# A sixth seven-product piece per group, and low parts made by ScalarE and an adding transfer, in a streaming-encoder block

## The chip, the core and the metric

The kernel runs on one core of a Trainium2 chip. The core has a matrix engine (TensorE, PE in the profile; its weight loads are listed apart as PEld), VectorE (DVE), ScalarE (ACT), GpSimd (POOL) and SyncE (SP). Each takes its own instructions in order, and they wait for each other by semaphores. Transfers between HBM and SBUF, or within SBUF, are issued from a queue of an engine (here SP's, for two small cases ACT's) and are carried by 16 transfer engines. Matmuls accumulate in PSUM, eight banks of 128 x 512 float32. The metric is the device time of one execution in microseconds.

## What is computed

One layer of an encoder on 256 tokens of width 2048, all in float32: a half feed-forward block, a mixer of two recurrent branches, cross-attention to 256 memory tokens, a second half feed-forward block, and a last norm. The change touches the two feed-forward blocks alone:

```python
DFF = 5632
def swiglu(h, w_up, w_down):
    gate, up = jnp.split(h @ w_up, 2, axis=-1)
    return (jax.nn.silu(gate) * up) @ w_down
...
x = x + 0.5 * swiglu(rms_norm(x, ffn1_norm[l]), ffn1_w_up[l], ffn1_w_down[l])
...
x = x + 0.5 * swiglu(rms_norm(x, ffn2_norm[l]), ffn2_w_up[l], ffn2_w_down[l])
return rms_norm(x, final_norm)
```

## The kernel before

**Float32 from two halves.** TensorE multiplies in the rounded type float32r. Every float32 operand v is therefore split into a high part h, v rounded to float32r, and a low part l = v - h. A product is three matmuls: high by high, low by high, high by low; low by low is dropped. `split` (line 119) does this: ScalarE copies v into h, VectorE subtracts h from v into l. `three` (line 421) issues the matmuls of a list of products: first, for each product, the weights' high part with the high and the low part of x; then, for each product, the weights' low part with the high part of x. So the low part of a weight piece is needed last.

**Pieces of weights.** All weights stream from HBM once, in pieces of 128 x 2048 float32, 1 MB. `plan` (line 127) lists them in order; `weights` (line 164) keeps two of them prepared ahead: before the matmuls of a piece are written out, those of the next are already split. `prepare` (line 181) issues the load into a `raw` buffer on SP's queue and then the split. There are three `raw`, three `h` and three `l` buffers (lines 71 to 73), and one `td`, one `tl` and one `ev` in the feed-forward blocks (line 321).

**A feed-forward block** (`ffn`, line 440). The 5632 hidden columns are taken in 11 groups of 512. A group's up projection runs over 8 pieces p; each holds 256 rows (two slices of 128) of 512 gate and 512 up columns, so with the two halves of the 256 tokens it is a 2 x 2 by 2 x 2 block product. `PRODUCTS` (line 433) names how a piece is multiplied:

- "plain" (group 0): the eight ordinary products.
- "fast": seven products of sums of blocks, after Strassen and Winograd. The sums of weight blocks are made by VectorE, three subtractions into `td` (lines 194 to 196), and `td` is split as well, into a second `h` buffer and `tl`. So a fast piece costs VectorE `td`, `l` (1536 wide), and `tl` (two halves of 1024); ScalarE copies 1536 + 2 x 1024.
- "mixed": eight products which add into the same accumulators as the seven-product kind, from the plain weight blocks with two extra operands of x (`less`). It costs the split of 2048 alone.

Both kinds add into seven accumulators, one PSUM bank each. Which product of which piece is the first and the last in an accumulator is in `uses` (line 444). At the end ScalarE and VectorE fold the seven accumulators into gate and up of both token halves and apply silu (lines 496 to 518): first, behind the last fast piece, accumulators 0, 5 and 4, which only fast pieces use (lines 504 to 506); the rest behind the group's last piece. The result is turned by eight transposes and split into two `hidop` tiles (`turn`, line 458), four pieces later.

The down projection of two earlier groups is spread between the groups: four down pieces of 24 matmuls follow each group's up pieces (line 54), adding to the residual `x` at line 532.

`ffn_order` (line 42) lays down the order. In groups 1 and 2 kinds alternate; from group 3 on it is 1, 0, 3, 4, 2, 5, 7, 6 with pieces 0, 2 and 6 mixed and 1, 3, 4, 5 and 7 fast.

**x operands.** For each pair of slices of x, `operand_pairs` (line 384) makes the split of x itself and what the kind needs beside it: `less` for mixed pieces, four sums for pieces of the "fast" kind. Piece 4 is mixed in groups 1 and 2 and fast from group 3 on, so pair 4 needs both sets, and its `less` goes to a slot of its own, `xd`. In the first block this runs at the start, between the first pieces (line 570), in the second between the pieces of the matmul before it.

**Order.** The first eight preparations are in an order written out by hand (`manual_schedule`, line 169). For the rest the compiler orders each engine's instructions by their place in the program and by when it expects their inputs and buffers; buffers are given out at compile time, and the waits are fixed with them.

Of the kernel before, what the change touches and what calls it, by code (L numbers as in the profile page):

```python
# [41 lines left out]
def ffn_order():  # L42

    out, down = [("plain", 0, p) for p in range(8)], [("down", 0, 1, c, 0) for c in range(4)]
    for g in range(1, NG):
        if g < 3:  # L50
            out += [(("mixed", "fast")[p % 2], g, p) for p in (0, 1, 2, 3, 5, 4, 7, 6)]
        else:
            out += [("mixed" if p in (0, 2, 6) else "fast", g, p) for p in (1, 0, 3, 4, 2, 5, 7, 6)]
        if g > 2 and g % 2:
            down = [("down", g - 2, 2, c, b) for c in range(4) for b in (g - 2, g - 1)]
        n = 2 if g < 3 else 4
        out, down = out + down[:n], down[n:]
    return out + [("down", NG - 2, 2, c, b) for c in range(4) for b in (NG - 2, NG - 1)]
# [3 lines left out]
def block_kernel(ctx: ExitStack, tc: tile.TileContext, xT, xin, memT, vec, gfin, bgate, lruw, wu1, wd1, win, wv,  # L62
# [24 lines left out]
    def slot(dt=F32, name="slot"):  # L87
        return slots.tile([P, 1024], dt, name=name, tag="slot")
# [41 lines left out]
    def plan_ffn(name, wu, wd):  # L130
        for e in orders[name]:
            src = wd[e[4], e[3]] if e[0] == "down" else wu[e[1], e[2]]
            plan.append(((name,) + e, src, e[0] == "fast"))

    def plan_columns(name, w, which):
        plan.extend(((name, i), w[i], False) for i in which)

    def plan_rows(name, w, g):
        plan.extend(((name, g, kq), w[g, kq], False) for kq in range(w.shape[1]))

    plan_ffn("ffn1", wu1, wd1)
    for hf in range(2):
# [21 lines left out]
    def weights(*key):  # L164
        while plan and len(ahead) < 2:
            i = next(planned)
            k, src, fast = plan.pop(0)
            if i == 0:
                in_turn.enter_context(tc.manual_schedule(engines={sp.engine, act.engine, dve.engine}))
            if i < len(head):  # L170
                head[i]()
            ahead.append((k, prepare(src, fast, 4 if i < 4 else 1)))
            if i in rest:
                rest[i]()
            if i == 7:
                in_turn.close()
        k, w = ahead.pop(0)
        assert k == key, (k, key)
        return w

    def prepare(src, fast, cuts=1):

        raw = rawp.tile([P, 2048], F32, name="raw", tag="raw")
        n = 2048 // cuts
        if not fast:
            h, l = split_tiles()
            for a in range(0, 2048, n):
                sp.dma_start(raw[:, a:a + n], src[:, a:a + n])
# [5 lines left out]
        dve.tensor_tensor(out=two[0], in0=raw[:, None, :512].broadcast_to([P, 2, 512]), in1=two[1], op=ALU.subtract)  # L194
        dve.tensor_tensor(out=td[:, 1024:1536], in0=raw[:, 1024:1536], in1=td[:, :512], op=ALU.subtract)
        dve.tensor_tensor(out=td[:, 1536:], in0=raw[:, 1536:], in1=td[:, 1024:1536], op=ALU.subtract)
# [184 lines left out]

    def operand_pairs(src, gain, q, xg, out):

        for a in src:
            i = len(out)
            g = xg[:, i * 512:(i + 1) * 512]
            for z in range(2):
                act.activation(g[:, z * T:][:, :T], a[:, z * T:(z + 1) * T], ACT.Copy,  # L390
                               scale=col(gain, 4 * q + 2 * i + z))
            h, l = slot(F32R, "xh"), slot(F32R, "xl")
            split(h[:, :512], l[:, :512], g)
            both = 2 * q + i == 4
            d = slot(F32R, "xd") if both else None
            less = None if i else (d[:, :256], d[:, 256:512]) if both else (h[:, 512:768], l[:, 512:768])
            out.append(((h, l), less))

        def sums():
            s = slot(name="xs")  # L400
            for i, ((h, l), less) in enumerate(out):
                a = [xg[:, i * 512 + j * P:][:, :P] for j in range(4)]

                def made(h, l, n, at, terms):
                    o = [s[:, at + j * P:][:, :P] for j in range(n)]
                    for j, (x, y, op) in enumerate(terms(o)):
                        dve.tensor_tensor(out=o[j], in0=x, in1=y, op=op)
                    split(h, l, s[:, at:at + n * P])

                if less:  # L410
                    made(*less, 2, 0, lambda o: ((a[0], a[1], ALU.subtract), (a[2], a[3], ALU.subtract)))
                if i or 2 * q + i == 4:
                    if not i:
                        s = slot(name="xs")
                    made(h[:, 512:], l[:, 512:], 4, 512 * i,
                         lambda o: ((a[1], a[3], ALU.add), (o[0], a[0], ALU.subtract),
                                    (a[1], a[0], ALU.subtract), (a[2], o[1], ALU.subtract)))

        return sums
# [20 lines left out]
    def ffn(name, pairs, sq, then, begin=(), sums=()):  # L440
# [38 lines left out]
        for at, e in enumerate(order):  # L479
# [3 lines left out]
            if kind != "down":  # L483
# [9 lines left out]
                                     u[0] == (p, i), u[-1] == (p, i)))  # L493
                three(products)
                last = at + 1 == len(order) or order[at + 1][1] != g or following == "down"
                if kind == "fast" and p == 7 or last:
                    if p == 7 or kind == "plain":
                        ev = scoped["ev"].tile([P, 2048], F32, name="ev", tag="ev")
                        e0, e1, e2, e3 = (ev[:, i * 512:(i + 1) * 512] for i in range(4))
                        if rstd is None:  # L500
                            with tc.issue_after(done["high"]):
                                rstd = sq.rstd_tokens()
                if kind == "fast" and p == 7:
                    act.activation(e0, accs[0], ACT.Copy)
                    dve.tensor_tensor(out=e1, in0=accs[5], in1=e0, op=ALU.add)
                    dve.tensor_tensor(out=e2, in0=accs[4], in1=e1, op=ALU.add)
                elif last:
                    if kind == "plain":
                        activate(e0, accs[0], accs[1], 0)
                        activate(e3, accs[3], accs[2], 1)  # L510
# [632 lines left out]
```

## Time and profile before

| | |
|---|---|
| median of three runs | 2471.65 us (2470.84 to 2472.26) |
| the profiled execution | 2472.93 us, its span 2471.1 us |
| granted TensorE clock, mean | 0.999 |
| loads from HBM | 472.17 MB read, 192 GB/s over the span |

The span is the time from the first to the last instruction in the trace; the rest of the execution lies around it. A group of instructions in the profile has the line and engine, the operation, the program's names of what it writes and reads, its shapes, how often it occurs, busy time in us and the mean in ns, and the idle time of its engine before it with what ended it. In the timeline the columns are the start and the length in us. The first feed-forward block fills about the first 700 us and the second the last 760 us; between them lie the mixer and the attention, with split pieces only.

### The profile page before, as it was taken

The numbers are of one execution on the slowest core, as the hardware profiler recorded it, in microseconds if no ns is written. First come the engines' busy times: TensorE is split into PE (matmuls) and PEld (weight loads), VectorE is DVE, ScalarE is ACT, GpSimd is POOL, SyncE is SP. The second block draws the span as 40 slices with busy tenths as digits, with TensorE's granted clock in tenths as the row PEclk, the third lists the DMA queues.
The fourth block names the chain that finished last, engine by engine and source line by source line (L and its number), as shares of the span: only waits on it lengthen the run. The fifth ranks groups of instructions, "written<-read, shape, count | busy, mean of one in ns | idle before, by whom it ended". The sixth has DMA issues, their size and how long they took to land.

```text
span 2471.1 us, 28936 instructions
## 1 busy us (share of the span) xinstructions
PE 2458.9 (100%) x11722; PEld 2055.4 (83%) x11722; DVE 1894.9 (77%) x1958; ACT 1304.3 (53%) x1321; POOL 0.2 (0%) x4
## 2 busy tenths in 40 slices
PE   9999999999999999999999999999999999999998
PEld 8788888888888888888888888888888888888887
DVE  7999989999765757567665676556589999999985
ACT  8555555555564444458434554555555555555553
POOL 0000000000000000000000000000000000000000
PEclk9999999999999999999999999999999999999999
DMA  8555555555655444454655565554555655555553
GB/s 294 187 201 192 203 204 204 204 195 199 212 178 190 169 171 171 169 185 176 219 178 197 195 209 185 175 171 156 184 191 187 205 204 204 202 195 201 203 200 141
DMA packets 70694, 476.15 MB, mean 193 GB/s; under 512 B 7840, under 2 KB 8096, under 8 KB 14752
## 3 DMA queue, kind: packets, MB, share of 16 engines
q1 hardware_dynamic: 69840, 473.17, 55.0%
q8 instruction: 92, 1.51, 0.2%
q10 hardware_dynamic: 720, 1.13, 0.1%
q14 instruction: 42, 0.34, 0.0%
HBM read 472.17 MB, written 2.10 MB: 192 GB/s over the span
## 4 chain that ended last, share of the span: by engine, by line
PE 95%; DVE 2%; ACT 1%; issue 1%; DMA 0%; SPq 0%; ACTq 0%; DVEq 0%
PE acc L424 17%; PE acc L425 17%; PE acc L427 17%; PE acc L212 11%; PE acc L233 8%; PE acc L234 8%; PE acc L236 8%; PE acc L216 5%; PE acc L463 1%; DVE l L121 1%; PE acc L749 1%; ACT h L120 1%; PE acc L370 1%; PE acc L1003 0%; DVE tl L121 0%
## 5 line engine op out<-in xcount | busy, mean ns | idle before, releaser
L121 DVE TENSOR_TENSOR l<-raw,h 128x2048 fp32r<-128x2048 f32 (+2 forms) x452 | 953.6, 2117 | 346.8 <-ACT h L120 340.8
L120 ACT ACTIVATE h<-raw 128x2048 fp32r<-128x2048 f32 (+2 forms) x452 | 802.5, 1778 | 665.5 <-PE acc L234 227.6
L424 PE MATMUL acc<-h,xh 128*128 128x512 f32 x1304 | 511.9, 393 | 2.1 <-ACT h L120 1.9
L425 PE MATMUL acc<-h,xl 128*128 128x512 f32 x1304 | 508.2, 390 | 0.0
L120 ACT ACTIVATE h<-td 128x1024 fp32r<-128x1024 f32 x192 | 197.7, 1053 | 253.9 <-DVE td L194 142.2
L233 PE MATMUL acc<-h,ops 128*128 128x512 f32 x832 | 326.9, 393 | 0.0
L234 PE MATMUL acc<-h,ops 128*128 128x512 f32 x832 | 324.4, 390 | 0.0
L424 PEld LDWEIGHTS acc<-h,xh 128*128 128x128 f32 x1304 | 245.4, 188 | 62.3 <-ACT h L120 10.7
L121 DVE TENSOR_TENSOR tl<-td,h 128x1024 fp32r<-128x1024 f32 x192 | 230.0, 1218 | 81.7 <-PE acc L427 53.3
L425 PEld LDWEIGHTS acc<-h,xl 128*128 128x128 f32 x1304 | 245.3, 188 | 50.3
L212 PE MATMUL acc<-ops,h 128*128 128x512 f32 x1152 | 277.8, 393 | 0.3
L424 PE MATMUL acc<-h,hidop 128*128 128x512 f32 x704 | 275.7, 392 | 0.0
L425 PE MATMUL acc<-h,hidop 128*128 128x512 f32 x704 | 274.3, 390 | 0.0
L212 PEld LDWEIGHTS acc<-ops,h 128*128 128x128 f32 x1152 | 211.9, 188 | 42.6 <-DVE ops L273 0.9
L427 PE MATMUL acc<-l,xh 128*128 128x512 f32 x920 | 237.5, 389 | 0.0
L236 PE MATMUL acc<-l,ops 128*128 128x512 f32 x832 | 205.8, 389 | 0.0
L427 PEld LDWEIGHTS acc<-l,xh 128*128 128x128 f32 x920 | 172.7, 188 | 36.0
L427 PE MATMUL acc<-l,hidop 128*128 128x512 f32 x704 | 188.3, 389 | 0.0
L236 PEld LDWEIGHTS acc<-l,ops 128*128 128x128 f32 x832 | 156.2, 188 | 32.4
L233 PEld LDWEIGHTS acc<-h,ops 128*128 128x128 f32 x832 | 156.3, 188 | 32.1
L234 PEld LDWEIGHTS acc<-h,ops 128*128 128x128 f32 x832 | 156.3, 188 | 31.5
L427 PEld LDWEIGHTS acc<-l,hidop 128*128 128x128 f32 x704 | 132.2, 188 | 27.5
(215 smaller groups left out, 2152.5 us busy)
## 6 DMA issues: line engine op xcount, KB each, us to landing
raw<-wu SPq DMA_DIRECT2D x172, 1024.0 KB, 4.9
raw<-wd SPq DMA_DIRECT2D x88, 1024.0 KB, 4.8
raw<-win SPq DMA_DIRECT2D x40, 1024.0 KB, 4.8
raw<-wg SPq DMA_DIRECT2D x32, 1024.0 KB, 4.8
raw<-wab SPq DMA_DIRECT2D x16, 1024.0 KB, 4.8
raw<-wout SPq DMA_DIRECT2D x16, 1024.0 KB, 4.8
raw<-wq SPq DMA_DIRECT2D x16, 1024.0 KB, 4.8
raw<-wk SPq DMA_DIRECT2D x16, 1024.0 KB, 4.8
```

The lines of the kernel that those rows point to most:

```text
L120: done["high"] = act.activation(h, raw, ACT.Copy).ins
L121: dve.tensor_tensor(out=l, in0=raw, in1=h.bitcast(F32), op=ALU.subtract)
L212: pe.matmul(acc, h[:, k * P:(k + 1) * P], xs[k], start=k == 0, stop=False)
L216: done["product"] = pe.matmul(acc[:, :T], l[:, k * P:(k + 1) * P], xs[k][:, :T], start=False, stop=k == KT - 1).ins
L233: pe.matmul(accs[t], x[:, t * P:][:, :P], h[j], start=first and j == 0, stop=False)
L234: pe.matmul(accs[t], x[:, T + t * P:][:, :P], h[j], start=False, stop=False)
L236: done["product"] = pe.matmul(accs[t], x[:, t * P:][:, :P], l[j], start=False, stop=last and j == 3).ins
L370: pe.transpose(accs[m // 2][:, m % 2 * T + t * P:][:, :P], tile[:, t * 512 + m * P:][:, :P], ident)
L424: pe.matmul(acc, ah, bh, start=start, stop=False)
L425: pe.matmul(acc, al, bh, start=False, stop=False)
L427: pe.matmul(acc, ah, bl, start=False, stop=stop)
L463: pe.transpose(acc[:, z * T + t * P:][:, :P], hid[t][:, (2 * y + z) * P:][:, :P], ident)
```

## The change

From group 3 on piece 2 becomes fast, so that only pieces 0 and 6 are mixed, and the order becomes 1, 3, 0, 4, 2, 6, 5, 7. All seven accumulators now end with piece 7, the group's last, and all folding steps come behind it (`ends` and `last` are both true there).

The two mixed pieces of these groups get the kind "added" in the plan. Their low part is not made by VectorE. `begin_added` loads the piece, lets ScalarE write its negative, rounded, into `l` (that is -h), and issues from GpSimd's queue a transfer within SBUF that adds `raw` to `l`, which leaves v - h. It is called one preparation earlier than before: the piece's load, negation and add stand ahead of the load and the split of the piece before it. The piece's own turn in `prepare` leaves only ScalarE's copy into `h`.

Since piece 2 is mixed in groups 1 and 2 and fast afterwards, pair 2 of x now needs both sets as well as pair 4; the two share the slot `xd`.

```diff
-            out += [("mixed" if p in (0, 2, 6) else "fast", g, p) for p in (1, 0, 3, 4, 2, 5, 7, 6)]
+            out += [("mixed" if p in (0, 6) else "fast", g, p) for p in (1, 3, 0, 4, 2, 6, 5, 7)]
...
-            plan.append(((name,) + e, src, e[0] == "fast"))
+            kind = "fast" if e[0] == "fast" else "added" if e[0] == "mixed" and e[1] > 2 else "plain"
+            plan.append(((name,) + e, src, kind))
...
+            if plan and plan[0][2] == "added":
+                begun.append(begin_added(plan[0][1]))
+            ahead.append((k, prepare(src, kind, 4 if i < 4 else 1)))
...
+    def begin_added(src):
+
+        raw = rawp.tile([P, 2048], F32, name="raw", tag="raw")
+        l = lp.tile([P, 2048], F32R, name="l", tag="l")
+        sp.dma_start(raw, src)
+        act.activation(l, raw, ACT.Copy, scale=-1.0)
+        nc.gpsimd.dma_start(l, raw, accum_op=ALU.add)
+        return raw, l
+
+    def prepare(src, kind, cuts=1):
+
+        if kind == "added":
+            raw, l = begun.pop(0)
+            h = hp.tile([P, 2048], F32R, name="h", tag="h")
+            done["high"] = act.activation(h, raw, ACT.Copy).ins
+            return h, l
...
+    BOTH = [2, 4]
...
-            both = 2 * q + i == 4
-            d = slot(F32R, "xd") if both else None
-            less = None if i else (d[:, :256], d[:, 256:512]) if both else (h[:, 512:768], l[:, 512:768])
+            less = None if i else (h[:, 512:768], l[:, 512:768])
+            if 2 * q + i in BOTH:
+                if 2 * q + i == BOTH[0]:
+                    xd.append(slot(F32R, "xd"))
+                n = 512 * BOTH.index(2 * q + i)
+                less = [xd[-1][:, a:a + 256] for a in (n, n + 256)]
...
-                if i or 2 * q + i == 4:
+                if i or 2 * q in BOTH:
...
-                if kind == "fast" and p == 7 or last:
-                    if p == 7 or kind == "plain":
+                ends = kind != "plain" and uses[g, 0][-1][0] == p
+                if ends or last:
+                    if ends or kind == "plain":
...
-                if kind == "fast" and p == 7:
+                if ends:
...
-                elif last:
+                if last:
```

More of the change, by code (lines that the diff above doesn't have):

```diff
@@ L132, in plan_ffn @@
             src = wd[e[4], e[3]] if e[0] == "down" else wu[e[1], e[2]]
-            plan.append(((name,) + e, src, e[0] == "fast"))
+            kind = "fast" if e[0] == "fast" else "added" if e[0] == "mixed" and e[1] > 2 else "plain"
+            plan.append(((name,) + e, src, kind))
     def plan_columns(name, w, which):
-        plan.extend(((name, i), w[i], False) for i in which)
+        plan.extend(((name, i), w[i], "plain") for i in which)
     def plan_rows(name, w, g):
-        plan.extend(((name, g, kq), w[g, kq], False) for kq in range(w.shape[1]))
+        plan.extend(((name, g, kq), w[g, kq], "plain") for kq in range(w.shape[1]))
     plan_ffn("ffn1", wu1, wd1)
@@ L166, in weights @@
             i = next(planned)
-            k, src, fast = plan.pop(0)
+            k, src, kind = plan.pop(0)
             if i == 0:
@@ L171, in weights @@
                 head[i]()
-            ahead.append((k, prepare(src, fast, 4 if i < 4 else 1)))
+            if plan and plan[0][2] == "added":
+                begun.append(begin_added(plan[0][1]))
+            ahead.append((k, prepare(src, kind, 4 if i < 4 else 1)))
             if i in rest:
@@ L179, in weights @@
         return w
-    def prepare(src, fast, cuts=1):
+    begun = []
+    def begin_added(src):
[11 more added lines that the diff above has]
+            return h, l
         raw = rawp.tile([P, 2048], F32, name="raw", tag="raw")
         n = 2048 // cuts
-        if not fast:
+        if kind == "plain":
             h, l = split_tiles()
@@ L377, in normed @@
             ops.add(accs[m // 2][:, m % 2 * T:][:, :T], col(gain, 4 * c + m))
+    BOTH = [2, 4]
+    xd = []
     def operand_pairs(src, gain, q, xg, out):
```

## The prediction

> **What bounds the kernel now.** I read the page's first and fourth parts, then busy time by stages, then single instructions of one group of the second feed-forward block.
>
> ```profile
> span 2471.1 us, 28936 instructions
> PE 2458.9 (100%) x11722; PEld 2055.4 (83%) x11722; DVE 1894.9 (77%) x1958; ACT 1304.3 (53%) x1321; POOL 0.2 (0%) x4
> PE 95%; DVE 2%; ACT 1%; issue 1%; DMA 0%; SPq 0%; ACTq 0%; DVEq 0%
> ```
>
> TensorE is busy for all but 12.2 us and carries 95% of the chain that ended last, so an instruction taken from it comes off the time, as long as nothing else becomes late. A busy engine here says only that its matmuls follow one another. What one costs is read from the distance of their starts:
>
> ```profile
> 2002.08 0.39 PE L424 MATMUL acc<-h,xh 128*128 128x512 f32 x1
> ...
> 2006.84 0.39 PE L424 MATMUL acc<-h,xh 128*128 128x512 f32 x1
> ...
> 2017.37 0.39 PE L424 MATMUL acc<-h,hidop 128*128 128x512 f32 x1
> ...
> 2022.81 0.39 PE L424 MATMUL acc<-h,hidop 128*128 128x512 f32 x1
> ...
> 2033.70 1.03 PE L463 MATMUL acc<-vt,ev 128*128 128x128 f32 x8
> 2034.49 0.48 PE L424 MATMUL acc<-h,hidop 128*128 128x512 f32 x1
> ```
>
> A fast piece has 21 matmuls and takes 2006.84 - 2002.08 = 4.76 us; a down piece has 24 and takes 5.44 us. Both give 0.227 us a matmul, though each row says 0.39: they overlap. A mixed piece has 24 too.
>
> The engine next in line is VectorE. The two windows are one group each (stretch, its length, busy time and count of PE, PEld, DVE, ACT and POOL, granted clock, DMA share, GB/s); below them stand VectorE's waits for `tl` from the timeline, the same one coming back after 63.14 us:
>
> ```profile
> 2000.00:2062.90 62.90, 62.90 (x281) 51.75 (x281) 56.77 (x53) 33.50 (x27) 0.00 (x0) 1.00 0.57 200
> 2062.90:2126.00 63.10, 63.09 (x282) 51.95 (x281) 56.93 (x53) 33.51 (x27) 0.00 (x0) 1.00 0.57 200
> ```
>
> ```profile
> 2034.13 2.36 DVE L121 TENSOR_TENSOR tl<-td,h 128x1024 fp32r<-128x1024 f32 x2 [1.98 <-ACT h L120]
> ...
> 2055.26 2.36 DVE L121 TENSOR_TENSOR tl<-td,h 128x1024 fp32r<-128x1024 f32 x2 [3.27 <-PE acc L427]
> ...
> 2097.27 2.36 DVE L121 TENSOR_TENSOR tl<-td,h 128x1024 fp32r<-128x1024 f32 x2 [2.00 <-ACT h L120]
> ...
> 2118.40 2.36 DVE L121 TENSOR_TENSOR tl<-td,h 128x1024 fp32r<-128x1024 f32 x2 [3.27 <-PE acc L427]
> ```
>
> TensorE has no gap; VectorE is busy 56.9 of 63.1 us (90%), and its longest idle, 3.27 us, is spent waiting for TensorE: VectorE is ahead, by little.
>
> **The change part by part.**
>
> *One product fewer per group.* Groups 3 to 10 of both blocks, 16 groups, have 3 mixed and 5 fast pieces, 3 x 8 + 5 x 7 = 59 products; after it 2 x 8 + 6 x 7 = 58. Three matmuls a product: 16 x 3 = 48 matmuls, 48 x 0.227 = **-10.9 us**, 0.68 us a group.
>
> *VectorE's work.* Piece 2 becomes fast, and the low parts of pieces 0 and 6 leave VectorE.
>
> ```profile
> L121 DVE TENSOR_TENSOR l<-raw,h 128x2048 fp32r<-128x2048 f32 x340 | 776.5, 2288 | 339.2 <-ACT h L120 336.3 <-ACT ops L269 2.0 <-ACT lo L245 0.5
> L121 DVE TENSOR_TENSOR tl<-td,h 128x1024 fp32r<-128x1024 f32 x192 | 230.0, 1218 | 81.7 <-PE acc L427 53.3 <-ACT h L120 28.4
> L121 DVE TENSOR_TENSOR l<-raw,h 128x1536 fp32r<-128x1536 f32 x96 | 168.1, 1751 | 7.7 <-ACT h L120 4.4 <-PE acc L427 3.0
> L194 DVE TENSOR_TENSOR td<-raw 128x1024 f32<-128x1024 f32 x96 | 117.0, 1218 | 1.3
> L196 DVE TENSOR_TENSOR td<-raw,td 128x512 f32<-128x512 f32 x96 | 66.0, 688 | 2.0
> L195 DVE TENSOR_TENSOR td<-raw,td 128x512 f32<-128x512 f32 x96 | 66.0, 687 | 1.9
> ```
>
> A fast piece costs 1.22 + 0.69 + 0.69 + 1.75 + 2 x 1.22 = 6.79 us, a mixed one 2.29. Out go 3 x 2.29 = 6.87, in comes 6.79: a group stays at 56.8 us, now of 62.5 (91%). The new order (fast, fast, mixed, fast, fast, mixed, fast, fast) asks VectorE for 13.6 us in 2 x 4.76 + 5.44 = 14.96 us of TensorE; before, the same three pieces asked 15.9 us. The middle of a group gets looser.
>
> *The seam between groups gets tighter.* Before, `accs` 0, 5 and 4 were folded while the last mixed piece ran; now all seven end with piece 7.
>
> ```profile
> L513 DVE TENSOR_TENSOR ev<-acc,ev 128x512 f32<-128x512 f32 x60 | 39.1, 678 | 0.0
> L456 DVE SCALAR_TENSOR_TENSOR ev<-ev,rtok 128x512 f32<-128x512 f32 x40 | 28.0, 740 | 0.0
> L532 DVE SCALAR_TENSOR_TENSOR x<-acc,x 128x512 f32<-128x512 f32 x96 | 65.6, 683 | 17.8 <-PE acc L427 17.6
> L468 DVE TENSOR_TENSOR hidop<-acc,hidop 128x512 fp32r<-128x512 f32 x44 | 28.3, 681 | 0.5 <-ACT hidop L467 0.5
> L505 DVE TENSOR_TENSOR ev<-acc,ev 128x512 f32<-128x512 f32 x20 | 13.6, 682 | 0.0
> L504 ACT ACTIVATE ev<-acc 128x512 f32<-128x512 f32 x20 | 11.6, 581 | 1.3 <-PE acc L427 1.1
> ```
>
> ```profile
> 2009.79 0.39 PE L427 MATMUL acc<-tl,xh 128*128 128x512 f32 x1
> 2010.17 0.50 PE L424 MATMUL acc<-h,xh 128*128 128x512 f32 x1
> ```
>
> One ScalarE step of 0.58 and two VectorE steps of 0.68 move 5.4 us later, behind the last product. TensorE needn't wait for them: the next down piece writes two banks, one was unused, the other is free after the 0.58 us, and is first written after 12 matmuls (2.7 us). But VectorE's work piles up. From the end of a group TensorE runs four down pieces, eight transposes and the first fast piece: 4 x 5.44 + 0.79 + 4.76 = 27.3 us. In it VectorE has nine folding steps (7 x 0.68 + 2 x 0.74 = 6.2), two `hidop` (1.4), four `x` (2.7), the first fast piece (6.8), all of the second but its `tl` (4.35) and four low parts (9.2): 30.6 us. Two of these low parts, 4.6 us, fit before the seam, in the time that the middle has gained; 26.0 us are left for 27.3. I put its cost at 0, with 1.3 us of room. Without that cover (one low part stays behind the seam, 2.3 - 1.3) it costs 1.0 us a group; the lower bound is -0.15 us a group, the gap in the two rows above (0.38 between starts instead of 0.23) behind today's fast pair, which may close.
>
> *The mixed pieces' low parts.* ScalarE writes -h into `l`, POOL's queue issues a transfer that adds `raw` to it, ScalarE later makes h.
>
> ```profile
> L120 ACT ACTIVATE h<-raw 128x2048 fp32r<-128x2048 f32 x340 | 650.6, 1914 | 509.0 <-PE acc L234 227.6 <-PE acc L212 81.4 <-issue 75.5
> L120 ACT ACTIVATE h<-td 128x1024 fp32r<-128x1024 f32 x192 | 197.7, 1053 | 253.9 <-DVE td L194 142.2 <-PE acc L425 100.4 <-DVE td L196 7.9
> L120 ACT ACTIVATE h<-raw 128x1536 fp32r<-128x1536 f32 x96 | 143.1, 1491 | 156.3 <-PE acc L425 151.2 <-issue 3.2 <-ACT hidop L467 1.0
> ```
>
> ```profile
> raw<-wu SPq DMA_DIRECT2D x172, 1024.0 KB, 4.9
> ...
> x<-xin SPq DMA_DIRECT2D x8, 256.0 KB, 8.2
> ```
>
> ```profile
> SPq L188 <- DVE l L121: 1201.7, 217, 16.4
> ```
>
> ScalarE: two more passes of 1.91 and a fast piece (1.49 + 2 x 1.05) in place of a 1.91: 33.5 + 3.8 + 3.6 - 1.9 = 39.0 of 62.5 us, hidden. No row has an adding transfer. A load of 1 MB lands 4.9 us after its issue and moves each byte twice (read, write); an add moves it three times (two reads, a write). Bounds: 4.9 us, as a load, and 4.9 + 8.2 = 13.1 us, a load behind the slowest median landing of the page. I take 9.8, two loads one after the other, as the transfer engines are at 0.57 already (two adds of two loads' work each lift that to about 0.57 x 16/12 = 0.76, twelve loads a group being today's work).
>
> How long has it? First use of `l` is the 17th matmul of its piece, 16 x 0.227 = 3.6 us in. `l` has three buffers. If they go round in turn, the second mixed piece gets the first's, free at that piece's end; then come two fast pieces: 9.5 + 3.6 - 1.9 of negation = **11.2 us** for the add. The first mixed piece gets the buffer of the third down piece and has 5.44 + 9.5 + 3.6 - 1.9 = 16.7 us. So 9.8 fits, by 1.4 us, and I price it at nothing. Every microsecond beyond 11.2 stops TensorE once a group, 16 us in all.
>
> The new waits: on ScalarE the negation waits for an `l` buffer, with the next fast piece's h behind it; POOL's queue has nothing else; on SP the mixed piece's load goes ahead of its neighbour's, and as a mixed piece keeps `raw` until its add has landed, two buffers serve the fast pieces: one load (4.9) and VectorE's reading (4.35) per buffer, a piece every 4.6 us against 4.76 that TensorE needs. Today SP waits for VectorE to free `raw` (the last row), so loads are early and this holds, barely.
>
> *Piece 2 needs both sets of x operands.* Once a block: four small steps and one 512-wide split more.
>
> ```profile
> 49.96 0.68 DVE L121 TENSOR_TENSOR xl<-xs,xh 128x512 fp32r<-128x512 f32 x1
> 50.57 0.28 DVE L407 TENSOR_TENSOR xs<-xg,xs 128x128 f32<-128x128 f32 x1
> 50.77 0.28 DVE L407 TENSOR_TENSOR xs<-xs,xg 128x128 f32<-128x128 f32 x1
> ```
>
> ```profile
> 60.00:70.00 10.00, 10.00 (x45) 8.26 (x44) 10.00 (x16) 5.73 (x8) 0.00 (x0) 1.00 0.41 147
> 70.00:80.00 10.00, 8.07 (x29) 5.45 (x28) 9.47 (x9) 5.81 (x5) 0.00 (x0) 0.90 0.56 178
> ```
>
> Steps start 0.20 us apart and a split takes 0.6 more: 4 x 0.2 + 0.6 = 1.4 us. In the first block VectorE is full at 60 to 70 us and TensorE loses 1.9 us right behind: I take **+1.4 us** (bounds 0 and 2.8, twice that). In the second it is free.
>
> *The sum.* The profiled execution took 2472.93 us, its span 2471.1 and 1.8 around it. 2472.93 - 10.9 + 1.4 = 2463.4; the median of the runs, 2471.65, lies 1.3 lower, so I forecast **2462.1**. With the bounds of the small terms (-16 x 0.15 - 1.4 and +1.4, and 0.15 us of new gaps a group) its own range is 2458 to 2466.
>
> **The rivals.**
>
> *The seam is too full.* For: 1.3 us of room, and VectorE at 90%. Against: it waits for TensorE today. At 0.6 us a group the gain is gone: 2462.1 + 9.6 = 2471.7. At the full 1.0 us it is 2478.
>
> *The adds land late (the other side).* Place: the 17th matmul of the second mixed piece. From 11.2 + 9.5 / 16 = 11.8 us behind the negation the kernel is slower. At the upper bound, 13 us: 2462.1 + 16 x 1.8 = 2491. For: no row prices an add or POOL's issue, and loads run beside it. Against: buffers freed earlier than in turn would give it up to 16.7 us. The Trainium skill speaks for it: "DMA: Bandwidth & Descriptors", section "Measured (HBM→SBUF, 128 partitions, SWDGE, issued from GpSimd)", has 6.15 us for 1 MB from POOL's queue, and "Collectives: The Full Stack", section "The bandwidth ceiling: the fold count and why AG ≠ RS ≠ AR", puts an add at half a copy's rate for its two source reads; an estimate from both is 12.3 us, 1.1 late, which would make 2480. No row here shows an add yet.
>
> *Adds are issued only where VectorE pauses.* VectorE's two pauses a group lie 42 us apart on one side (2055.26 to 2097.27). An add issued at a random point there would wait some 19 us: 19 + 9.8 - 11.2 = 17.6 late, 16 x 17.6 = 282, 2744 us. Against: the kernel has no transfer of POOL's, so the trace is silent. The Trainium skill, "SBUF — State Buffer", section "Who interferes with whom", says that VectorE's two-port modes block the writing of POOL's descriptors, and infers that a tensor_tensor, all there is in these stages, does not.
>
> **How the numbers follow.** Forecast 0.57 (2458 to 2466); seam 0.18, of it 0.05 still faster, 0.09 within, 0.04 slower; adds late 0.20, of it 0.02 within and 0.18 slower; pauses 0.05. A measurement of this kernel can tell 0.2%, 4.9 us, from no change. Faster 0.57 + 0.05 = 0.62, same 0.09 + 0.02 = 0.11, slower 0.04 + 0.18 + 0.05 = 0.27. The range 2458 to 2486 holds the forecast, the seam and about a third of the late adds, 0.57 + 0.18 + 0.07 = 0.82.
>
> **What would show it.** Right: 48 fewer matmuls in the three lines of `three`, the group's repeat at 62.5 us, VectorE still near 57 us a group, DMA share near 0.76 there, no wait of TensorE on the adding transfer. Wrong: a wait of PE or PEld on a DMA into `l` once a group (adds late, or pauses, if POOL's issue is long); PE waiting on h or `tl` in the group's first two fast pieces (seam); SP's loads waiting for `raw` behind an add and ScalarE waiting for them. A repeat that stays at 63.1 us with VectorE idle nowhere would refute the budget itself.

## The result, and the profile after

| | before | after |
|---|---|---|
| median of 20 runs each | 2471.72 us (2470.58 to 2472.37) | 2467.34 us (2466.17 to 2468.29) |
| the profiled execution | 2472.93 us, span 2471.1 us | 2467.42 us, span 2465.3 us |

The change takes 4.4 us off the median, a ratio of 0.9983 (95% interval 0.9976 to 0.9990). It is faster, by 0.18%, and by less than half of the 9.5 us forecast. From the page of the kernel after, its head, and a row each from the parts on the chain and on DMA issues:

```profile
span 2465.3 us, 29124 instructions
PE 2446.9 (99%) x11674; PEld 2044.5 (83%) x11674; DVE 1896.5 (77%) x2016; ACT 1393.1 (57%) x1387; POOL 28.1 (1%) x36
...
PE 92%; DVE 3%; ACT 2%; DMA 2%; issue 1%; SPq 0%; ACTq 0%; DVEq 0%
...
l<-raw POOLq DMA_DIRECT2D x32, 1024.0 KB, 11.0
```

The matmuls are 48 fewer, TensorE's share of the chain falls from 95 to 92%, and its busy time by 12.0 us. But it is idle for 2465.3 - 2446.9 = 18.4 us where it was idle for 12.2. So 6.2 us were given back. (Of the 12.0 us, 48 x 0.227 = 10.9 are the matmuls; most of the rest is a stretch at half clock which the profiled execution of before has, 1.2 us, shown at the end.) The windows show where that wasn't, and where it was. One group of the second block, cut as in the prediction (stretch, its length, busy time and count of PE, PEld, DVE, ACT and POOL, granted clock, DMA share, GB/s):

```profile
2105.89:2168.25 62.36, 62.36 (x280) 51.43 (x279) 57.03 (x56) 39.04 (x32) 1.73 (x2) 1.00 0.76 236
```

Here everything is as forecast: no idle TensorE, VectorE at 57 us, ScalarE at 39, a DMA share of 0.76. Three other windows of the kernel after, and the same three of the kernel before:

```profile
50.00:100.00 50.00, 46.94 (x206) 36.90 (x205) 48.92 (x61) 32.59 (x32) 0.00 (x0) 1.00 0.55 189
...
150.00:200.00 50.00, 47.48 (x212) 38.45 (x211) 44.08 (x47) 29.70 (x26) 1.87 (x2) 1.00 0.70 217
...
1900.00:2000.00 100.00, 97.69 (x433) 79.09 (x432) 89.92 (x91) 61.19 (x50) 3.48 (x4) 1.00 0.73 219
```

```profile
50.00:100.00 50.00, 48.07 (x206) 38.53 (x206) 47.92 (x57) 32.30 (x31) 0.00 (x0) 0.97 0.58 197
...
150.00:200.00 50.00, 49.75 (x223) 40.43 (x222) 48.03 (x48) 27.06 (x25) 0.00 (x0) 1.00 0.53 177
...
1900.00:2000.00 100.00, 100.00 (x447) 81.95 (x447) 93.42 (x90) 52.63 (x44) 0.00 (x0) 1.00 0.55 193
```

TensorE's idle time grows by 1.13 us in the first stretch, by 2.27 in the second and by 2.31 in the third: 5.7 of the 6.2 us. The first is the start, with pair 2's second set of operands; but there the kernel before ran its stretch at half clock (0.97 in its row), and both kernels start 206 matmuls in these 50 us, so against that execution this idle time is no loss. The other two hold group 3 of each block, the first group with adding transfers; the groups behind it have no idle time. What happens there stands in the chain of waits of the kernel after (start, length, what ran or was waited for):

```profile
157.06 1.91 ACT l L191
...
159.30 12.29 DMA l<-raw
171.64 4.75 DMA raw<-wu
...
178.23 1.05 ACT h L120
...
187.05 0.49 PE acc L449
```

and in the timelines of its SP queue, of ScalarE and of VectorE:

```profile
159.51 0.33 SPq L210 DMA_DIRECT2D raw<-wu  x1
171.64 0.33 SPq L190 DMA_DIRECT2D raw<-wu  x1
172.06 3.79 SPq L210 DMA_DIRECT2D raw<-wu  x2
```

```profile
176.41 1.92 ACT L191 ACTIVATE l<-raw 128x2048 fp32r<-128x2048 f32 x1 [5.45 <-DMA raw<-wu]
```

```profile
179.29 2.36 DVE L121 TENSOR_TENSOR tl<-td,h 128x1024 fp32r<-128x1024 f32 x2 [3.84 <-ACT h L120]
```

The first mixed piece's negation starts at 157.06 and its add goes out at 159.30. The add lands 12.29 us later, and until then holds its `raw` buffer. SP issues one fast piece's load meanwhile, at 159.51. Next in its queue is the load of the second mixed piece (L190), which waits for an add's buffer: it goes out at 171.64, and behind it, from 172.06 on, go the loads of fast pieces (L210). ScalarE stands for 5.45 us in front of the second negation, with the next fast piece's h behind it (178.23). That piece had been loaded, and VectorE, done with its `td` by 175.5, stands for 3.84 us until its h is there; TensorE waits for h up to 187.05. So the chain runs from the add's buffer over the mixed piece's load and the order on ScalarE. The fast load that stands behind the mixed one in SP's queue isn't on it. The waits of SP for an add, from the list of waits of the kernel after (in all, times, longest):

```profile
SPq L207 <- DMA l<-raw: 51.8, 15, 5.6
...
SPq L210 <- DMA l<-raw: 40.5, 14, 4.0
...
SPq L190 <- DMA l<-raw: 23.2, 2, 11.7
```

Loads of other pieces (fast ones L210, plain ones L207) wait for adds in the other groups too, at most 5.6 us, and TensorE has no idle time there. The load of a mixed piece does so just twice, once a block, for 11.7 us at most. That is the theory to test; its rivals are that the first group loses the time in the seam, on VectorE, or because the adds themselves land late.

### The profile page after: what moved, and what is told of

Its sections match the earlier page's. It is cut to its first block, busy times and chain, and to the rows that moved or that the text cites. A ratio compares the mean times of both kernels' runs of the same rounds, so it can differ in the third digit from the quotient of the medians.

```text
span 2465.3 us, 29124 instructions
## 1 busy us (share of the span) xinstructions
PE 2446.9 (99%) x11674; PEld 2044.5 (83%) x11674; DVE 1896.5 (77%) x2016; ACT 1393.1 (57%) x1387; POOL 28.1 (1%) x36
## 3 DMA queue, kind: packets, MB, share of 16 engines
q10 hardware_dynamic: 720, 1.13, 0.1%
## 4 chain that ended last, share of the span: by engine, by line
PE 92%; DVE 3%; ACT 2%; DMA 2%; issue 1%; SPq 0%; ACTq 0%; DVEq 0%
PE acc L452 16%; PE acc L449 16%; PE acc L450 16%; PE acc L231 11%; PE acc L252 8%; PE acc L253 8%; PE acc L255 8%; PE acc L235 5%; ACT h L120 1%; DMA raw<-wu 1%; DVE l L121 1%; PE acc L775 1%; PE acc L488 1%; PE acc L389 1%; DMA l<-raw 0%
## 5 line engine op out<-in xcount | busy, mean ns | idle before, releaser
L121 DVE TENSOR_TENSOR l<-raw,h 128x2048 fp32r<-128x2048 f32 (+2 forms) x420 | 874.8, 2085 | 334.7 <-ACT h L120 331.2
L120 ACT ACTIVATE h<-raw 128x2048 fp32r<-128x2048 f32 (+2 forms) x420 | 734.6, 1752 | 557.8 <-PE acc L253 227.1
L449 PE MATMUL acc<-h,xh 128*128 128x512 f32 x1280 | 500.3, 391 | 6.8 <-ACT h L120 6.7
L450 PE MATMUL acc<-h,xl 128*128 128x512 f32 x1280 | 497.7, 389 | 0.0
L120 ACT ACTIVATE h<-td 128x1024 fp32r<-128x1024 f32 x224 | 235.8, 1055 | 241.5 <-DVE td L213 103.5
L121 DVE TENSOR_TENSOR tl<-td,h 128x1024 fp32r<-128x1024 f32 x224 | 273.1, 1222 | 83.5 <-ACT h L120 54.5
L449 PEld LDWEIGHTS acc<-h,xh 128*128 128x128 f32 x1280 | 240.2, 188 | 61.7 <-ACT h L120 11.1
L450 PEld LDWEIGHTS acc<-h,xl 128*128 128x128 f32 x1280 | 240.3, 188 | 49.2
L452 PE MATMUL acc<-l,xh 128*128 128x512 f32 x832 | 217.7, 389 | 0.0
L452 PEld LDWEIGHTS acc<-l,xh 128*128 128x128 f32 x832 | 156.0, 188 | 32.7 <-DVE l L121 0.3
```

Of the source, the lines that this page charges most:

```text
L120: done["high"] = act.activation(h, raw, ACT.Copy).ins
L121: dve.tensor_tensor(out=l, in0=raw, in1=h.bitcast(F32), op=ALU.subtract)
L449: pe.matmul(acc, ah, bh, start=start, stop=False)
L450: pe.matmul(acc, al, bh, start=False, stop=False)
L452: pe.matmul(acc, ah, bl, start=False, stop=stop)
```

## The experiments

Each kernel is the changed one with an edit. Ratios are to the kernel before, run beside it on the same chip, with the 95% interval.

**Adds from group 4 on, in the order of the change.**

```diff
-            kind = "fast" if e[0] == "fast" else "added" if e[0] == "mixed" and e[1] > 2 else "plain"
+            kind = "fast" if e[0] == "fast" else "added" if e[0] == "mixed" and e[1] > 3 else "plain"
```

> The changed kernel, but in group 3 of both blocks VectorE makes the low parts of the two mixed pieces, as before; from group 4 on ScalarE and the adding transfer. Theory 1 (buffer): the 2.3 us that TensorE idles in group 3 of each block arise because the load of the second mixed piece waits on SP for the raw buffer that the first add holds until it lands. Then TensorE's idle in 150 to 200 us falls from 2.5 to under 0.5 us, in 1900 to 2000 us from 2.3 to under 0.5, and the time is 2467.3 - 4.6 = 2462.7 us. Rival (VectorE is late at this place, whoever holds a buffer): VectorE gets 4.6 us more work in group 3, the idle stays at 2.3 us or grows, the time is 2467 us or more.

2472.55 us, ratio 1.0002 (0.9994 to 1.0011): a miss. The idle time didn't go; it went to the group that now has the first adds. Windows of this kernel:

```profile
150.00:200.00 50.00, 49.94 (x224) 41.03 (x223) 49.32 (x51) 25.72 (x24) 0.00 (x0) 1.00 0.50 176
200.00:250.00 50.00, 47.65 (x205) 38.20 (x204) 43.81 (x44) 29.49 (x25) 1.87 (x2) 0.97 0.76 231
1900.00:2000.00 100.00, 98.06 (x437) 79.65 (x436) 93.42 (x93) 55.18 (x47) 1.73 (x2) 1.00 0.64 203
2000.00:2100.00 100.00, 98.40 (x434) 79.81 (x433) 91.33 (x88) 60.73 (x49) 1.72 (x2) 1.00 0.71 228
```

Group 3 of the first block is all but free now, its group 4 loses 2.35 us (and has a stretch at half clock, 0.97), and in the second block the loss is spread over two windows. So the place isn't tied to group 3 and its change of order, but to the start of the adds. The wait is another one, though: in this group 4 no mixed piece's load waits for an add. A fast piece's load does, for 3.3 us; it goes out at 235.48 and lands 7.03 us later, and ScalarE's h waits for it. The whole kernel is some 5 us slower than the change. Group 3 now has the new order with all low parts on VectorE, which by a run below costs 1.95 us a group, 3.9 us for the two blocks; the rest isn't placed.

**The order and kinds of before, with pair 2's second operands alone.**

```diff
-            out += [("mixed" if p in (0, 6) else "fast", g, p) for p in (1, 3, 0, 4, 2, 6, 5, 7)]
+            out += [("mixed" if p in (0, 2, 6) else "fast", g, p) for p in (1, 0, 3, 4, 2, 5, 7, 6)]
...
-            kind = "fast" if e[0] == "fast" else "added" if e[0] == "mixed" and e[1] > 2 else "plain"
+            kind = "fast" if e[0] == "fast" else "added" if e[0] == "mixed" and e[1] > 99 else "plain"
```

> The kernel before, with the second set of operands made for pair 2 as well (nothing reads it there); order, products and low parts as before. Theory: VectorE is full from 40 to 80 us of the first block, so 1.4 us more of work stops TensorE for 1.1 to 1.4 us: 2471.7 + 1.3 = 2473.0 us, TensorE's idle in 0 to 100 us up from 3.0 to about 4.3. Rival (the loss at the start has another source, such as the granted clock): 2471.7, idle as before.

2472.48 us, ratio 1.0004 (0.9995 to 1.0012); the time doesn't resolve it. In the profile TensorE is busy for 47.09 us of the window from 50 to 100, where the kernel before has 48.07: 1.0 us more idle time. But it starts 207 matmuls there, where the kernel before, with its stretch at half clock, starts 206. So the second set leaves TensorE idle for about 1.0 us at the start, and what that costs in time isn't shown.

**The second sets later.** In the first block the second sets of pairs 2 and 4 go from the places of their pairs to nine places further on in the list of what runs between the first pieces.

```diff
...
-        rest[i] = lambda q=q: sums1[q]()
+        rest[i] = lambda q=q: sums1[q]("early" if 2 * q in BOTH else "all")
+    for q, i in ((1, 16), (2, 17)):
+        rest[i] = lambda q=q: sums1[q]("late")
```

> The changed kernel, with the second sets of pairs 2 and 4 of the first block made behind the 16th and 17th piece instead of the 7th and 8th. Theory: VectorE's 2.8 us for them go from a place where it is full to one where TensorE covers them; idle in 0 to 100 us falls from 4.4 to between 1.6 and 3.0, the time to 2464.5 to 2466 us. Rival (VectorE has no room there either, at 92% of 100 to 150 us): the same idle appears at 100 to 150 us, 2467 us.

2465.81 us, ratio 0.9973 (0.9963 to 0.9984), 6.2 us under the kernel before beside it where the change gave 4.4. The window from 50 to 100 is back at 48.13 us, and the next stays full. The intervals of the two ratios overlap, and this window has a stretch at half clock too (0.97); but it starts 209 matmuls where the change, at full clock, starts 206. So the start's 1.1 us of idle time are had back. Pair 4's second set, which the kernel before also makes early, has moved with pair 2's.

**No lead for the added pieces.** Load, negation and add are issued in the piece's own turn.

```diff
-            if plan and plan[0][2] == "added":
-                begun.append(begin_added(plan[0][1]))
+            if kind == "added":
+                begun.append(begin_added(src))
```

> The changed kernel, with load, negation and add of a mixed piece in its own turn instead of one preparation earlier. In the changed kernel 15.8 us lie between the end of the second negation and the first matmul with its low part, 17.3 us for the first; an add lands 11.0 us after its issue. One fast piece less, 4.76 us, leaves 11.0 and 12.5. If an add needs all its 11 us (theory): TensorE waits for the adding transfer by 0 to 1.3 us a group, 2467 to 2488 us, and the idle of group 3 changes with the buffers. If the compiler puts the negation as early as its inputs allow whatever the place in the program (rival): 2467 us, the same distances.

2488.43 us, ratio 1.0063 (1.0051 to 1.0076), some 21 us above the change, 1.3 us for each of 16 groups. But an add that is late, the wait that was expected, is a small part of it: TensorE waits 2.2 us in all for an add into `l`, and 13.8 us, in 26 waits, for h. From the lists of waits of this kernel, SP's and ScalarE's:

```profile
SPq L190 <- DMA l<-raw: 96.4, 16, 7.0
```

```profile
ACT h L120 <- DMA raw<-wu: 78.1, 24, 5.3
...
ACT l L191 <- DMA raw<-wu: 5.6, 8, 1.9
```

Now the mixed piece's load waits for an add in all 16 groups, but the negation hardly waits for that load: 5.6 us, where the change has 31.7. What ScalarE waits for here is loads whose h it makes directly, 78.1 us where the change has 10.1. One of them, a fast piece's, went out at 2006.96, behind an add of 2004.93, and landed after 8.54 us; the kernel before has 4.9 at the median. So here, too, loads come late beside the adds, but by another way than in the change's group 3.

**Four `raw` buffers.** The room comes from two slots of x operands.

```diff
-    rawp = pool("raw", 3)
+    rawp = pool("raw", 4)
...
-    slots = pool("slots", 24)
+    slots = pool("slots", 22)
```

> The changed kernel with four raw buffers instead of three, and 22 instead of 24 slots to make room. Theory (raw buffer): in the first group with adds the load of the second mixed piece gets a buffer that no add holds; SP's wait for an add at that load (23.2 us in 2 cases in the changed kernel) is gone, TensorE's idle in 150 to 200 and 1900 to 2000 us falls from 2.5 and 2.3 to under 0.5 us each, and the time falls by up to 4.6, to 2463 us, unless the two slots fewer cost time in the middle of the kernel. Rival (VectorE or ScalarE is late in that group for want of time, not of a buffer): the idle stays at 2 us a block, 2467 us.

2465.21 us, ratio 0.9974 (0.9964 to 0.9984). In its list of waits no mixed piece's load (L190) waits for an add any more. Windows of this kernel:

```profile
50.00:100.00 50.00, 45.87 (x192) 35.64 (x192) 46.55 (x61) 31.51 (x30) 0.00 (x0) 0.97 0.50 172
...
150.00:200.00 50.00, 49.24 (x218) 39.78 (x217) 45.30 (x48) 28.64 (x24) 1.86 (x2) 1.00 0.75 232
...
1900.00:2000.00 100.00, 100.00 (x448) 82.28 (x447) 93.27 (x93) 63.66 (x53) 3.47 (x4) 1.00 0.77 235
```

The idle time of the second block's group 3 is gone, that of the first block's falls from 2.5 to 0.8 us, with the order of the change as it was: most of the idle time of these groups hangs on the buffer that an add holds. The start pays: 4.1 us idle from 50 to 100, where the change has 3.1, and 192 matmuls for 206, with a stretch at half clock. The two slots taken away are the likely reason; that wasn't tried alone.

**The queue's order in group 3 alone.** There the mixed piece's load, negation and add are issued behind the preparation of the fast piece before it, not ahead of it. The number of buffers, the adds and the work stay.

```diff
+            soon = plan and plan[0][2] == "added"
+            if soon and plan[0][0][2] > 3:
                 begun.append(begin_added(plan[0][1]))
             ahead.append((k, prepare(src, kind, 4 if i < 4 else 1)))
+            if soon and plan[0][0][2] == 3:
+                begun.append(begin_added(plan[0][1]))
```

> The changed kernel, but in group 3 alone the load, negation and add of a mixed piece stand behind those of the fast piece before it, not ahead; later groups as changed. Theory (queue): what costs is that the fast piece's load stands behind the waiting load on SP; put ahead of it, it lands in time, and the idle of 2.5 and 2.3 us in the first group of each block falls to under 1 us each: 2464 to 2465 us. Rival (buffer, wherever the load stands; or the lead that is lost): idle as before or larger, as in the kernel without the lead (1.3 us a group): 2467 to 2469 us.

2462.04 us, ratio 0.9963 (0.9950 to 0.9976): 9.4 us under the kernel before, and 5.3 under the change's median (5.0 when each is held against the kernel before beside it), and 2 us less than the theory expected. From the timelines of the SP queue, ScalarE and GpSimd, and the windows of this kernel:

```profile
159.36 7.92 SPq L213 DMA_DIRECT2D raw<-wu  x2
172.01 0.33 SPq L193 DMA_DIRECT2D raw<-wu  x1
```

```profile
178.20 1.92 ACT L194 ACTIVATE l<-raw 128x2048 fp32r<-128x2048 f32 x1 [0.46 <-DMA raw<-wu]
```

```profile
163.92 1.00 POOL L195 DMA_DIRECT2D l<-raw  x1 [163.47 <-DVE td L216]
```

```profile
150.00:200.00 50.00, 50.00 (x225) 40.83 (x223) 45.73 (x49) 30.48 (x26) 1.87 (x2) 1.00 0.71 217
...
1900.00:2000.00 100.00, 99.44 (x446) 81.99 (x445) 91.68 (x91) 64.05 (x52) 3.48 (x4) 1.00 0.77 232
```

The mixed load is issued no earlier, at 172.01 where it was 171.64. But two fast loads (here L213) are now ahead of it, ScalarE makes the fast piece's h first and stands 0.46 us in front of the negation in place of 5.45, and the idle time is gone in the first block and down to 0.56 us in the second. The edit moves three things at once: the order on SP, the order on ScalarE, and the first add, which goes out at 163.92 where it was 159.30, well behind the fast load of 159.36 and not just ahead of one. No run separates them. By the chain of the change it was ScalarE that passed the wait on: what cost the time there was a load that couldn't go, with the h behind its negation that could have been made.

**The product without the adds, and the adds without the product.** First, the order and kinds of the change, with the low parts of all mixed pieces made by VectorE:

```diff
-            kind = "fast" if e[0] == "fast" else "added" if e[0] == "mixed" and e[1] > 2 else "plain"
+            kind = "fast" if e[0] == "fast" else "added" if e[0] == "mixed" and e[1] > 99 else "plain"
```

> Six fast pieces a group and the new order, but every low part by VectorE: no negation, no adding transfer. VectorE then needs 56.8 + 2 x 2.29 = 61.4 us of the 62.4 us of a group. Theory (the adds are what makes the sixth fast piece pay): VectorE sets the group's time; with 1 to 4 us of waits that it can't avoid, 62.4 to 65.4 us a group, 2467 + 0 to 48, most likely 2480 to 2495 us. Rival (VectorE's room was enough): the group repeats after 62.4 us without stalls, 2462 to 2467 us.

Then the order and five fast pieces of before, with adds for its three mixed pieces:

```diff
-            out += [("mixed" if p in (0, 6) else "fast", g, p) for p in (1, 3, 0, 4, 2, 6, 5, 7)]
+            out += [("mixed" if p in (0, 2, 6) else "fast", g, p) for p in (1, 0, 3, 4, 2, 5, 7, 6)]
...
-    BOTH = [2, 4]
+    BOTH = [4]
```

> Five fast pieces a group, order and x operands of the kernel before, but the low parts of the three mixed pieces from group 3 on by negation and adding transfer. VectorE is relieved of 6.9 us a group, TensorE has as many matmuls as before. Theory (TensorE sets the time): no gain but the gap of 0.15 us a group (2.4 us), and the first groups with adds stall as in the changed kernel (4.6 us): 2469 to 2474 us. Rival (VectorE was already a bound): 2460 us or less.

The product alone: 2489.04 us, ratio 1.0072 (1.0058 to 1.0085). The adds alone: 2466.44 us, ratio 0.9979 (0.9970 to 0.9988). The first is as expected; the second lies 2.6 us below the range that was expected, and above its rival's. The repeat of a group is read from its eight transposes, here from the timelines of TensorE after, with the product alone and with the adds alone, one kernel a fence, two groups running:

```profile
2032.18 1.03 PE L488 MATMUL acc<-vt,ev 128*128 128x128 f32 x8
...
2094.54 1.03 PE L488 MATMUL acc<-vt,ev 128*128 128x128 f32 x8
```

```profile
2043.53 1.03 PE L488 MATMUL acc<-vt,ev 128*128 128x128 f32 x8
...
2107.84 1.03 PE L488 MATMUL acc<-vt,ev 128*128 128x128 f32 x8
```

```profile
2028.87 1.03 PE L488 MATMUL acc<-vt,ev 128*128 128x128 f32 x8
...
2091.64 1.03 PE L488 MATMUL acc<-vt,ev 128*128 128x128 f32 x8
```

62.36, 64.31 and 62.77 us, where the kernel before has 63.14. Without the adds the sixth fast piece makes VectorE the bound, and a group is 1.17 us longer than before for all its three matmuls fewer:

```profile
2000.00:2100.00 100.00, 98.92 (x429) 78.22 (x428) 96.28 (x87) 56.78 (x47) 0.00 (x0) 1.00 0.59 201
```

(a window of the kernel with the product alone: VectorE 96% busy). The adds alone save 0.37 us a group with the same matmuls, and TensorE has no idle time from 150 to 200, where its first group with adds runs: the stall that was expected there doesn't come.

**The change once more, and with both mends.** A second run of the changed kernel as a measure for the last one, which has the queue's order in group 3 and the late second sets together:

> The changed kernel once more, beside the next one on the same chip: 2467.3 us, 4.4 below the kernel before.

> Both remedies in the changed kernel: in group 3 the mixed piece's load, negation and add behind the fast piece before it, and the second sets of pairs 2 and 4 of the first block behind the 16th and 17th piece. If the two losses are separate, their gains add: 5.3 (first group) + 1.9 (start) below the changed kernel, 2460 us, with TensorE's idle under 3.2 us in 0 to 100 us and under 1 us in the first group of each block. If relieving one place only moves the wait to the other: 2462 us.

The change: 2467.60 us, ratio 0.9986 (0.9977 to 0.9995). With both: 2460.02 us, ratio 0.9953 (0.9940 to 0.9967), 11.1 us under the kernel before and 7.6 under the change on the same chip. Its windows have TensorE at 48.14 us from 50 to 100 (at 0.97, like the late second sets alone), 50.00 from 150 to 200, and 99.36 from 1900 to 2000: by these each mend returns what it did alone. It is the fastest of all kernels here.

## Why the prediction was right, and where it failed

The steady groups went as forecast; the sum did not. 2467.34 us is 5.2 us above the 2462.1 that were forecast, and outside the forecast's own range of 2458 to 2466. It lies within the whole range, 2458 to 2486, since that was drawn to hold the seam and a third of the late adds as well, and neither took place. That it does is luck: what filled the room was a loss that the sum has at nothing.

**The product: right.** A group repeats after 62.36 us in place of 63.14. Of the 0.78 us, 0.68 are the three matmuls; the rest is what two gaps between matmuls, one gone and one new, leave over (next but one).

**VectorE, ScalarE, DMA share: right.** 57.0 and 39.0 us a group and 0.76, as forecast, in the window after.

**The seam: right in price, by luck.** There is a new gap at the seam, at the group's last fast piece and not in the next group's first two, where the prediction looked for it. Timeline of TensorE after, last fast piece and first down piece:

```profile
2077.73 0.39 PE L450 MATMUL acc<-h,hidop 128*128 128x512 f32 x1
2078.08 0.73 PE L452 MATMUL acc<-tl,xh 128*128 128x512 f32 x2
2078.65 0.39 PE L449 MATMUL acc<-h,hidop 128*128 128x512 f32 x1
```

Starts 0.35 apart, then two rows in 0.57 us: 0.24 us more than three starts at 0.227, since `tl` comes late: VectorE makes its second half from 2076.81 to 2078.03, behind a low part of a down piece. It is paid by the gaps that went: the adds alone show that 0.37 us of a group of before were lost to VectorE, while TensorE read as busy without a break. The prediction had seen 0.15 of that. With 0.68 and 0.37 off and 0.24 on, 63.14 us come to 62.33, and 62.36 were measured. So the price of nothing holds because two gaps nearly cancel, and not for the 1.3 us of room that it was put down to.

**The adds' price: mis-sized, and harmless to the matmuls that use them.** Forecast were 9.8 us, between 4.9 and 13.1. Two rows of the view of tile `l` after, second block (POOL's issues: min/median/max in ns, first and last start; then landing times):

```profile
L192 POOL DMA_DIRECT2D l<-raw x16: 859/866/887, 1907.1 to 2364.6; - x16
...
DMA to landing us min/median/max: 8.0/11.0/12.3
```

The Trainium skill's estimate in the prediction, from the sections named there of "DMA: Bandwidth & Descriptors" and "Collectives: The Full Stack", was 12.3: the slowest adds reach it, the median doesn't. At 11.0 the forecast's room of 11.2 us would nearly have been used up. The room was larger. Timelines of the kernel after, ScalarE and TensorE, for a second mixed piece:

```profile
1986.47 1.92 ACT L191 ACTIVATE l<-raw 128x2048 fp32r<-128x2048 f32 x1 [0.36 <-DMA raw<-wu]
```

```profile
2004.23 1.98 PE L452 MATMUL acc<-l,xh 128*128 128x512 f32 x8
```

From the end of the negation, 1986.47 + 1.92, to the first use are 15.8 us: the `l` buffers don't go round in turn, as the prediction had allowed among its reasons against this rival. No matmul of the change waited for an add, so adds that land late for their reader decided nothing. What their flight cost is the buffer that they read, below.

**Adds issued only where VectorE pauses: refuted.** POOL's issue took 0.87 us at the median and 0.89 at most in the rows just shown, with VectorE busy for 57.0 of 62.4 us. By the inference in the Trainium skill, "SBUF — State Buffer", section "Who interferes with whom", a tensor_tensor doesn't stop it; the trace agrees. (The prediction called it all there is in these stages; its own rows have scalar_tensor_tensor too, for `ev` and `x`.)

**The start: right in idle time, not shown in the time.** Forecast were +1.4 us; TensorE's idle time there grew by 1.1, and by 1.0 with the second set alone. Both are held against an execution of before that had its stretch at half clock there, and the time of the second set alone (2472.48 us, the kernel before beside it 2472.05) doesn't resolve it.

**The new waits: the step that failed.** The prediction said of SP's loads, "loads are early and this holds, barely", and priced them at nothing. Its sum for this was a rate, 4.6 us a piece against 4.76, with 4.9 us for a load, and in the steady groups TensorE indeed has no idle time. In the group where the adds begin, once a block, two things were otherwise. The load of the second mixed piece had to wait itself, for up to 11.7 us, as its buffer was held by an add, for 12.3 us and not for the forecast 9.8. And a load beside an add could land late: in the second block that of a fast piece, issued at 1907.50 with an add out since 1907.06, landed after 9.48 us. ScalarE passed the waits on. The prediction had seen that on ScalarE the negation has the next fast piece's h behind it, but had it wait for an `l` buffer; it waited for its load, and h, VectorE and TensorE waited with it. This cost 2.3 us of idle TensorE in each block, 4.6 us in all, most of the 5.2 that separate forecast and result.

Turning the order in those two groups brought some 5 us. Not all of it read as idle time: the two windows show 2.5 and 1.8 us, and TensorE's busy time fell by 1.0 (2446.9 to 2445.9). These are gaps between starts, as the counts of the windows show: 225 and 446 matmuls started in place of 212 and 433, 26 more, 5.9 us of work at 0.227, of which the windows behind give back 0.7 (224 for 225 from 200 to 250 us, 447 for 449 from 2000 to 2100). That this kernel comes to 2462.04 us, where 2462.1 was forecast, is chance: with the late second sets as well it is 2460.02. The prediction's last part did name the sign, SP's loads waiting for `raw` behind an add and ScalarE waiting for them, but no term of the sum and no rival stood for it.

**Left open.** Why a mixed load meets an add's buffer in the first group of the change only, and never with the adds alone: buffers are given out at compile time, and the runs show which wait it is, not why it was given. And which of the three things that the order in group 3 moves brings its gain.

## What to carry to other kernels

When an asynchronous transfer takes over an engine's work, price the buffer that it holds, for its whole flight, and not only the time until its result is wanted. Follow that buffer to the next load that wants it, and then to whatever stands in order behind that load: other loads in its queue, and, on the engine that reads it first, work for pieces that are already there. Another order cost nothing here, where another buffer took room from something else. Look at the first group of such a pattern by itself, since a rate that holds in the steady groups says nothing about its start.

## What the runs showed of the hardware

**A busy TensorE at 100% can hide gaps.** A row of 512 columns lasts 0.39 us while starts come 0.227 apart, so a gap under about 0.16 us between starts doesn't show as idle time. The kernel before had no idle time in its groups and yet 0.37 us a group to give, as the adds alone showed.

**A stretch at half clock behind a short stall.** In the profiled execution of before TensorE stood for 1.69 us up to 76.37 us, and soon after ran at half clock. Rows of its timeline, and a window:

```profile
76.37 0.50 PE L424 MATMUL acc<-h,xh 128*128 128x512 f32 x1 [1.69 <-ACT h L120]
...
77.78 1.12 PE L427 MATMUL acc<-tl,xh 128*128 128x512 f32 x2 [0.22 <-DVE tl L121]
78.70 0.63 PE L424 MATMUL acc<-h,xh 128*128 128x512 f32 x1
79.13 0.63 PE L425 MATMUL acc<-h,xl 128*128 128x512 f32 x1
```

```profile
79.00:80.00 1.00, 1.00 (x4) 0.71 (x4) 1.00 (x1) 1.00 (x2) 0.00 (x0) 0.50 0.98 418
```

Six starts from 78.70 to 81.26 are 0.43 us apart and not 0.227, which costs 1.2 us, about what this execution took above the median of before (2472.93 to 2471.72). The profiled execution of after has a stall of 1.67 us at the same place and no half clock behind it. So it doesn't come each time; the windows of other runs above that read 0.97 have such a stretch too. What triggers it stays open. The Trainium skill, "TensorE: Matmul & The Clock Gate", section "What's actually happening", puts the half clock behind an idle window of some 3.4 us; here one execution shows it behind stalls of 1.69 and 0.22 us, with none of that length ahead of them, and the measurement decides.
